# Weights in 512 KB pieces, one account for VectorE's time, tables without GpSimd, final loads one stage ahead

## The chip, the core and the metric

The kernel runs on one core of a Trainium2 chip. The core has TensorE (PE) for matmuls, VectorE (DVE), ScalarE (ACT), GpSimd (POOL) and a queue engine, SyncE (SP); each takes its own instructions in order, and they wait for each other by semaphores. SP, ACT and POOL also start DMA transfers. The metric is the device time of one execution in microseconds (us), lower is better.

## What is computed

One decoder block on 512 tokens of width 2048, in float32, and then a final norm:

```python
h = rmsnorm(x, norm1_g);  z = h @ w_in                     # 2048 -> 3328
x = x + concat([gated(zu, zv), attention(zq, zk, zvv)]) @ w_out
h2 = rmsnorm(x, norm2_g)
q = h2 @ w_query                                           # 8 heads, two halves of 128
s1, s2 = q[..., 0, :] @ sub_keys[0].T, q[..., 1, :] @ sub_keys[1].T
v1, i1 = top_k(s1, 16); v2, i2 = top_k(s2, 16)
top_v, flat = top_k(v1[:, None] + v2[None, :], 16)         # of 256 sums
experts = i1[flat // 16] * 128 + i2[flat % 16]             # of 16384
gates = softmax(top_v)
a = gelu(h2 . expert_down[experts])
out = rmsnorm(x + sum(gates * a * expert_up[experts]), norm_f_g)
```

Each token has 8 x 16 = 128 experts of its own.

## The kernel before

**Two ways to the experts.** 352 of the 512 tokens (three blocks of 128 less 32) go through all 16384 experts densely: 128 "down" blocks of 128 experts each give activations, which are multiplied by a table of gates (zero for an expert that the token did not choose) and go into 16 "up" chunks of 8 blocks. The first 128 tokens and the last 32 gather their own rows instead: 640 "units" (`unit`, line 688), each a gather of 128 rows of 4 KB started on GpSimd (`fetch_to`, 682) and one operation of 1024 elements on VectorE (696 for down, 708 for up).

**Weights.** `Stream` (93) loads every weight matrix in pieces of 1 MB on SP into two buffers, `LOAD` = 2 ahead (104). Each piece is split in halves of 1024 columns: ScalarE makes the rounded part `whi` (118), VectorE or GpSimd the residual `wlo` (120), and `mm3` (141) multiplies three times for each pair of operands, lines 144 to 146. `get` (127) splits two halves ahead of use. A buffer is loaded anew when both of its halves are split. `on_pool` (181) says by the half's number which residuals are GpSimd's.

**Order.** The program is written out in one order by hand; each engine follows it. Stages: input projection with attention and gating; output projection of block 0 (`project`, 539); query of block 0; output projection of blocks 1 to 3; their query; down blocks 0 to 55; up chunks 0 to 5; then up chunks with the down blocks that they need between them; last the norm of the columns just finished (`rows_out`, 1181), 512 at a time, within the last up chunk. `NPRE` = 56 is the number of down blocks ahead of the first up chunk; their activations go through DRAM (`a_dram`), and `OPEN` = `NPRE` - 5 is the block after which the buffers of the tables are given up.

**Filling.** Small work between the matmuls is put in by two queues. `Filler.tick(budget)` (58) runs steps until their stated costs use up a budget of us given at each call (2.0 for each weight half in the query of block 0, 4.0 in the next stage, 2.4 for each half of a down block). The steps are the choice of the 16 best (`choose`, 585), the decoding of the choice into expert numbers (`decode`, 600), and the gate tables (`table`, 875). `Flow.step` (80), called by `mm3` with the nominal time of its three matmuls (`COL_NS` = 0.4505 ns for a column), runs the units at a fixed rate: one for each 2600, later 5200 and 4800 ns, and from block `OPEN` on at the rate that spreads them over what is left (`pace`, 1220).

**Tables.** A table is made four tokens at a time (`quad`, 889; 88 in all): VectorE compares the second key with `iota` (898), GpSimd multiplies by the gates (901), VectorE (905) or ScalarE (910, 912), by turns, makes the one-hot of the first key; TensorE multiplies them (918), ScalarE copies the result out (931). At block `OPEN` what is left of these steps is run at once (the loop at 1240).

**The end.** After down block 127 `open_last` (1146) and `finish_first` (1195) load the residual rows and the gathered sums of the first block on SP, add and normalize them; `finish_last` (1205) does the same for the last 32 tokens and is the last unit.

## Time and profile before

| | |
|---|---|
| time before, median of 3 runs | 3179.93 us (3173.95 to 3181.99) |
| the profiled execution, its own time | 3170.0 us |
| its span, first to last instruction | 3168.0 us |
| mean granted TensorE clock | 0.959 |
| TensorE busy | 2908.4 us, 92% |
| VectorE, ScalarE, GpSimd busy | 2318.6, 1133.9, 1672.8 us |
| moved by DMA | 801.85 MB, mean 253 GB/s |

The profile is of one execution. Matmuls are pipelined, so TensorE counts as busy while one is in flight; whether it runs at its pace is seen in the number of matmuls in a stretch. The stretches below are cut where the first matmul of each stage starts. A granted clock of 1.00 is 2.4 GHz, one of 0.50 is 1.2 GHz.

### The profile page before, as it was taken

How to read it: one execution, taken by the hardware profiler on the slowest of the kernel's cores; microseconds unless marked ns; L12 is line 12 of the kernel's file. 1: busy time of each engine (PE TensorE's matmuls, PEld its weight loads, DVE VectorE, ACT ScalarE, POOL GpSimd, SP SyncE). 2: the span in 40 equal slices, each digit the busy share in tenths (PEclk: the TensorE clock that was granted, in tenths of full speed). 3: DMA queues.
4: the chain of work that ended last, by engine and by line, in shares of the span. 5: the costliest groups of instructions: out<-in, count | busy, mean ns of one | idle time of the engine just before them, and what ended most of it. 6: DMA issues, size and time to landing. Idle time of an engine off the chain costs nothing. (4 is left out here: it accounts for less than half of the span.)

```text
span 3168.0 us, 43607 instructions
## 1 busy us (share of the span) xinstructions
PE 2908.4 (92%) x16925; PEld 2748.2 (87%) x16925; DVE 2318.6 (73%) x3218; ACT 1133.9 (36%) x1776; POOL 1672.8 (53%) x1071
## 2 busy tenths in 40 slices
PE   7999977888999999888999999999999999999955
PEld 6878755668999999888999999999999998999955
DVE  3126546865999999996778887777877776777744
ACT  3244444323333445453432223332332323323323
POOL 2133133365555778886655656556555565565522
PEclk9999989999999999987999999999999999999978
DMA  4211255575567666656998898888988888888862
GB/s 188 92 68 67 81 216 210 198 286 209 200 229 249 232 223 232 250 212 240 342 360 324 333 344 315 314 304 321 338 307 315 320 310 305 334 317 307 320 243 73
DMA packets 215359, 801.85 MB, mean 253 GB/s; under 512 B 19952, under 2 KB 80688, under 8 KB 165296
## 3 DMA queue, kind: packets, MB, share of 16 engines
q1 hardware_dynamic: 107504, 416.02, 36.3%
q0 software_dynamic: 92160, 335.59, 28.0%
q10 hardware_dynamic: 15488, 47.46, 3.9%
q8 instruction: 132, 2.16, 0.3%
q14 instruction: 75, 0.61, 0.1%
HBM read 753.98 MB, written 45.01 MB: 252 GB/s over the span
## 5 line engine op out<-in xcount | busy, mean ns | idle before, releaser
L120 POOL TENSOR_TENSOR wlo<-wraw,whi 128x1024 fp32r<-128x1024 f32 x269 | 684.3, 2546 | 923.4 <-ACT whi L118 818.5
L118 ACT CAST whi<-wraw 128x1024 fp32r<-128x1024 f32 x692 | 700.8, 1047 | 707.2 <-PE up L145 410.8
L120 DVE TENSOR_TENSOR wlo<-wraw,whi 128x1024 fp32r<-128x1024 f32 x423 | 662.4, 1572 | 306.7 <-ACT whi L118 304.9
L144 PE MATMUL up<-gah,whi 128*128 128x352 f32 x2048 | 668.7, 327 | 48.2 <-ACT whi L118 32.9
L146 PE MATMUL dn<-h2d,wlo 128*128 128x352 f32 x2048 | 670.2, 327 | 36.3 <-POOL wlo L120 25.6
L146 PE MATMUL up<-gah,wlo 128*128 128x352 f32 x2048 | 664.2, 324 | 11.2 <-POOL wlo L120 6.1
L145 PE MATMUL dn<-h2d,whi 128*128 128x352 f32 x2048 | 668.8, 327 | 0.0
L144 PE MATMUL dn<-h2d,whi 128*128 128x352 f32 x2048 | 665.4, 325 | 3.0 <-ACT whi L118 3.0
L145 PE MATMUL up<-gal,whi 128*128 128x352 f32 x2048 | 662.8, 324 | 0.0
L144 PEld LDWEIGHTS up<-gah,whi 128*128 128x128 f32 x2048 | 388.5, 190 | 56.1 <-ACT whi L118 34.0
L146 PEld LDWEIGHTS dn<-h2d,wlo 128*128 128x128 f32 x2048 | 390.0, 190 | 42.9 <-POOL wlo L120 29.8
L146 PEld LDWEIGHTS up<-gah,wlo 128*128 128x128 f32 x2048 | 388.3, 190 | 15.2 <-POOL wlo L120 8.1
L144 PEld LDWEIGHTS dn<-h2d,whi 128*128 128x128 f32 x2048 | 390.6, 191 | 3.3 <-ACT whi L118 3.3
L145 PEld LDWEIGHTS dn<-h2d,whi 128*128 128x128 f32 x2048 | 389.7, 190 | 0.0
L145 PEld LDWEIGHTS up<-gal,whi 128*128 128x128 f32 x2048 | 389.4, 190 | 0.0
L682 POOL DMA_INDIRECT row<-in_down_rows,idx x228 | 276.3, 1212 | 136.9 <-DVE row L696 60.9
L696 DVE SCALAR_TENSOR_TENSOR row<-row,half_row 128x1024 f32<-128x1024 f32 x228 | 273.9, 1211 | 43.7 <-DMA row<-in_down_rows,idx 30.3
L682 POOL DMA_INDIRECT row<-in_up_rows,idx x160 | 183.2, 1145 | 86.5 <-DVE half_row L708 35.7
L901 POOL TENSOR_TENSOR p<-eq,gT 128x1024 fp32r<-128x1024 bf16 x88 | 190.6, 2176 | 44.4 <-DVE eq L898 41.7
L682 POOL DMA_INDIRECT more<-in_up_rows,idx x160 | 170.5, 1066 | 72.2 <-DVE half_row L708 36.2
L708 DVE SCALAR_TENSOR_TENSOR half_row<-more,wgt,half_row 128x1024 f32<-128x1024 f32 x160 | 205.2, 1282 | 1.4
L708 DVE SCALAR_TENSOR_TENSOR half_row<-row,wgt,half_row 128x1024 f32<-128x1024 f32 x156 | 200.2, 1284 | 1.4
(218 smaller groups left out, 3963.5 us busy)
## 6 DMA issues: line engine op xcount, KB each, us to landing
wraw<-in_down SPq DMA_DIRECT2D x128, 1024.0 KB, 6.1
wraw<-in_up SPq DMA_DIRECT2D x128, 1024.0 KB, 6.6
wraw<-in_wout SPq DMA_DIRECT2D x32, 1024.0 KB, 4.8
wraw<-in_wq SPq DMA_DIRECT2D x32, 1024.0 KB, 4.8
wraw<-in_win SPq DMA_DIRECT2D x26, 1024.0 KB, 4.8
g_dram<-stage ACTq DMA_DIRECT2D x22, 1024.0 KB, 6.8
g<-g_dram SPq DMA_DIRECT2D x32, 704.0 KB, 9.7
aa<-a_dram SPq DMA_DIRECT2D x56, 176.0 KB, 9.2
```

The costliest lines, as they stand in the source:

```text
L118: self.nc.scalar.copy(hi, src)
L120: eng.tensor_sub(lo, src, hi.bitcast(F32))
L144: nc.tensor.matmul(ps, wh, xh, start=start, stop=False)
L145: nc.tensor.matmul(ps, wh, xl, start=False, stop=False)
L146: nc.tensor.matmul(ps, wl, xh, start=False, stop=stop)
L682: nc.gpsimd.indirect_dma_start(out=t, out_offset=None, in_=src, in_offset=bass.IndirectOffsetOnAxis(ap=idx[i][:, j, h:h + 1], axis=0))
L696: nc.vector.scalar_tensor_tensor(t, t, 1.0, half_row, op0=OP.mult, op1=OP.mult, accum_out=dots[i][:, j, h:h + 1])
L708: nc.vector.scalar_tensor_tensor(half_row, t, wgt[i][:, j:j + 1], half_row, op0=OP.mult, op1=OP.add)
L901: nc.gpsimd.tensor_tensor(p2, eq[:, :, None, :].to_broadcast([P, 4, 2, P]), hl[:, four, :, None].to_broadcast([P, 4, 2, P]), op=OP.mult)
```

## The change

1. `Stream` loads halves: pieces of 512 KB in four buffers, four ahead; a buffer is loaded anew when its half is split.
2. `Filler` and `Flow` go; `Pace` keeps an account for VectorE. Each `mm3` adds 0.97 of its nominal time (at most 3000 ns may stand), each piece of VectorE work takes off its stated cost. While the account is above zero it runs a unit if one is due (`gap`), else a step of the `hot` queue (choices, and the decoding of block 0). Steps of the `paced` queue (decoding and tables of blocks 1 to 3, 110 in all) run one in a step when `due` has reached `every` and nothing is hot, whatever the account. Residuals after the input projection go to GpSimd when VectorE's account is at or below zero and GpSimd's own is not below zero.
3. A quad makes its product of one-hot and gates in four operations on VectorE, none on GpSimd, and all one-hots of the first key on ScalarE.
4. `NPRE` goes from 56 to 80, so `OPEN` from 51 to 75.
5. The loads of the final norm go from SP to ACT; the work of the first block comes in the second quarter of the last up chunk, that of the last tokens is loaded in the third and done in the fourth. A second set of four buffers takes half of the partial sums.

The core of the diff follows. Left out are the removed classes `Filler` and `Flow`, the removal of their calls and the adapted costs of the steps (1750, 1750, 2950 for a choice; 2500, four times 3900, 1500 for a decoding), and the charges for other VectorE work (690 for a residual row or a transposed quarter, 2600 for a norm, 1060 for a table product, 520 for a sum).

```diff
 NCHUNK = NK // CB
-NPRE = 56
+NPRE = 80
 OPEN = NPRE - 5
 TG = 32
 NTG = TD // TG
...
+class Pace:
+        self.hot, self.paced, self.units = deque(), deque(), deque()
+        self.vector = self.pool = self.wait = self.due = 0.0
+        self.gap = 2600.0
+        self.every = 0.0
+    def spend(self, ns):
+        self.vector -= ns
+    def use_pool(self):
+        if self.vector > 0.0 or self.pool < 0.0:
+            self.vector -= 1250.0
+            return False
+        self.vector -= 500.0
+        self.pool -= 2500.0
+        return True
+    def run(self, q):
+        ns, f = q.popleft()
+        self.vector -= ns
+        r = f()
+        if r is not None:
+            self.later.append(r)
+    def step(self, ns):
+        self.vector = min(self.vector + 0.97 * ns, 3000.0)
+        self.pool = min(self.pool + ns, 3000.0)
+        self.wait += ns
+        self.due += ns
+        if self.paced and self.due >= self.every and not self.hot:
+            self.due -= self.every
+            self.run(self.paced)
+        while self.vector > 0.0:
+            if self.units and self.wait >= self.gap:
+                self.wait = max(self.wait - self.gap, -self.gap) if self.wait < 2 * self.gap else 0.0
+                self.vector -= 1260.0
+                self.pool -= 1100.0
+                self.units.popleft()()
+            elif self.hot:
+                self.run(self.hot)
+            else:
+                break
+    def turn(self):
...
+    def finish(self):
+        while self.hot or self.paced or self.later:
+            self.turn()
+            while self.hot:
+                self.run(self.hot)
+            while self.paced:
+                self.run(self.paced)
...
     def drain(self):
+        while self.units:
+            self.units.popleft()()
...
-    LOAD, SPLIT = 2, 2
+    LOAD, SPLIT = 4, 2
...
-        while self.loaded < min(n, len(self.chunks)):
-            i = self.loaded
-            self.raw[i] = self.pool.tile([P, 2048], F32, name="wraw", bufs=2)
-            self.nc.sync.dma_start(self.raw[i], self.chunks[i])
+        while self.loaded < min(n, 2 * len(self.chunks)):
+            p = self.loaded
+            self.raw[p] = self.pool.tile([P, 1024], F32, name="wraw", bufs=4)
+            self.nc.sync.dma_start(self.raw[p],
+                                   self.chunks[p // 2][:, (p % 2) * 1024:(p % 2 + 1) * 1024])
             self.loaded += 1
...
-            self.load(p // 2 + 1)
-            src = self.raw[p // 2][:, (p % 2) * 1024:(p % 2 + 1) * 1024]
+            self.load(p + 1)
+            src = self.raw.pop(p)
...
-            if p % 2:
-                del self.raw[p // 2]
-                self.load(p // 2 + 1 + self.LOAD)
+            self.load(p + 1 + self.LOAD)
...
-        flow.step(3 * ps.shape[-1] * COL_NS)
+        pace.step(3 * ps.shape[-1] * COL_NS)
...
-    LEAD, REST, ASK, EXPERTS = 52, 52 + 68, 52 + 96, 52 + 128
 
     def on_pool(p):
-        if p < LEAD:
+        if p < 52:
             return p < 4 or 20 <= p < 36
-        if p < REST:
-            return p % 3 == 2
-        if p < ASK:
-            return p % 2 == 0
-        if p < EXPERTS + 2 * OPEN:
-            return p % 4 != 0 if p < EXPERTS else p % 2 == 0
-        return p % 3 == 0
+        return pace.use_pool()
...
-            flow.q.append(unit(u))
+            pace.units.append(unit(u))
...
-                    for step in choose(psc, key[b], top[b], pos[b], 2 * g + h, s, h):
-                        fill.add(*step)
+                    pace.hot.extend(choose(psc, key[b], top[b], pos[b], 2 * g + h, s, h))
...
         def quad(n):
             def f():
+                turn()
                 t, hl = eT[0]
                 if len(ready) == 4:
                     take()
                 p1 = pear.tile([P, 4, P], F32R, name="p1", bufs=4)
-                eq = pear.tile([P, 4, P], BF16, name="eq", bufs=4)
                 p2 = pear.tile([P, 4, 2, P], F32R, name="p2", bufs=4)
-                four = slice(4 * n, 4 * n + 4)
-                nc.vector.tensor_tensor(eq, iota[:, None, :].to_broadcast([P, 4, P]),
-                                        t[:, 1, four, None].to_broadcast([P, 4, P]),
-                                        op=OP.is_equal)
-                nc.gpsimd.tensor_tensor(p2, eq[:, :, None, :].to_broadcast([P, 4, 2, P]),
-                                        hl[:, four, :, None].to_broadcast([P, 4, 2, P]),
-                                        op=OP.mult)
-                if n % 2 == 0:
-                    nc.vector.tensor_tensor(p1, iota[:, None, :].to_broadcast([P, 4, P]),
-                                            t[:, 0, four, None].to_broadcast([P, 4, P]),
-                                            op=OP.is_equal)
-                else:
-                    for j in range(4):
-                        nc.scalar.activation(p1[:, j, :], iota, AF.Abs, scale=-1.0,
-                                             bias=t[:, 0, 4 * n + j:4 * n + j + 1])
-                    nc.scalar.activation(p1, p1.bitcast(F32), AF.Relu, bias=1.0, scale=-1.0)
+                for j in range(4):
+                    k = 4 * n + j
+                    nc.vector.scalar_tensor_tensor(
+                        p2[:, j], iota[:, None, :].to_broadcast([P, 2, P]), t[:, 1, k:k + 1],
+                        hl[:, k, :, None].to_broadcast([P, 2, P]),
+                        op0=OP.is_equal, op1=OP.mult)
+                for j in range(4):
+                    nc.scalar.activation(p1[:, j, :], iota, AF.Abs, scale=-1.0,
+                                         bias=t[:, 0, 4 * n + j:4 * n + j + 1])
+                nc.scalar.activation(p1, p1.bitcast(F32), AF.Relu, bias=1.0, scale=-1.0)
...
+        plan, waiting = [], []
+            choice, steps = decoding(b)
+            turn, quads = table(b, choice)
+            head = [*steps, (600.0, lambda t=turn: t)]
+            n = len(head) if b == 0 else 0
+            plan += head[:n]
+            if b:
+                at = len(plan) - 24
+                for k, f in enumerate(head):
+                    plan.insert(at + 3 * k, f)
+            plan += [(0.0, lambda: None)] * 0 + [(1900.0, f) for f in quads]
+        pace.paced.extend(plan)
+        pace.every = OPEN * 48 * TD * COL_NS * 0.95 / len(plan)
...
+            if last and q == 1:
+                rest_of_first()
+            if last and q == 2:
+                pace.drain()
+                rest_of_last = finish_last()
+            if last and q == 3:
+                rest_of_last()
             if last and q:
                 rows_out(q - 1)
...
-            nc.sync.dma_start(t, x_dram[b + 1])
+            nc.scalar.dma_start(t, x_dram[b + 1])
...
-        nc.sync.dma_start(y, y_dram[0])
-        nc.sync.dma_start(x, x_dram[0])
-        nc.vector.tensor_add(y, y, x)
-        for q in range(4):
-            square(ND, P, y, q, nc.gpsimd)
-        last_norm(ND, P, y, o_rows[0])
+        nc.scalar.dma_start(y, y_dram[0])
+        nc.scalar.dma_start(x, x_dram[0])
+
+        def rest():
+            nc.vector.tensor_add(y, y, x)
+            for q in range(4):
+                square(ND, P, y, q, nc.gpsimd)
+            last_norm(ND, P, y, o_rows[0])
+        return rest
 
     def finish_last():
...
+    def spread():
         left = sum(2 * 24 for k, i in order if k == "d" and i >= OPEN)
         left += sum(384 for k, i in order if k == "u")
+        pace.gap = (left * TD * COL_NS - 45e3) / len(pace.units)
...
-            while fill.q or fill.later or ready:
-                fill.tick(1e9)
+            pace.finish()
+            while ready:
                 take()
             open_late()
-            pace()
+            spread()
             opening.extend([
...
-            finish_first()
-            flow.q.append(finish_last)
-    flow.drain()
+            rest_of_first = finish_first()
+    pace.drain()
```

## Rows read from the trace of the kernel before

**Rows 1.** The page's part 1: busy time of each engine, its share of the span, and its instructions.

```profile
PE 2908.4 (92%) x16925; PEld 2748.2 (87%) x16925; DVE 2318.6 (73%) x3218; ACT 1133.9 (36%) x1776; POOL 1672.8 (53%) x1071
```

**Rows 2.** Busy time of one stretch: its start and end (us from the span's start) and length, busy us and number of instructions of each engine, granted TensorE clock, busy share of the DMA engines, GB/s. It is one undisturbed up chunk: 384 matmuls of 352 columns.

```profile
2072.00:2133.00 61.00, 61.00 (x384) 61.00 (x383) 44.26 (x46) 18.57 (x23) 33.59 (x26) 1.00 0.82 312
```

**Rows 3.** The same view by stage. In order: output projection of the first token block; its query; output projection of the other three blocks; the first 56 expert-down blocks, and of these the flush of the tables; six expert-up chunks in a row; nine more of these with 72 down blocks between; the last up chunk; the end.

```profile
389.50:491.39 101.89, 75.08 (x283) 54.09 (x282) 53.98 (x52) 47.30 (x62) 35.54 (x14) 0.92 0.60 216
491.39:573.02 81.63, 61.29 (x232) 43.78 (x230) 65.08 (x144) 37.54 (x43) 28.39 (x11) 0.90 0.55 199
573.02:726.36 153.34, 134.00 (x548) 104.23 (x547) 114.13 (x198) 43.54 (x63) 75.71 (x51) 0.93 0.68 251
886.30:1503.60 617.30, 559.72 (x3404) 548.85 (x3403) 573.59 (x748) 283.23 (x585) 457.31 (x238) 0.91 0.66 234
1389.50:1457.20 67.70, 48.74 (x213) 44.47 (x212) 63.89 (x38) 35.08 (x105) 59.11 (x28) 0.54 0.32 128
1503.60:1896.00 392.40, 374.53 (x2306) 368.15 (x2305) 317.55 (x474) 126.86 (x164) 224.55 (x154) 1.00 0.90 341
1896.00:3026.40 1130.40, 1114.15 (x6914) 1109.12 (x6913) 858.39 (x917) 358.11 (x438) 638.42 (x460) 0.99 0.84 317
3026.40:3145.90 119.50, 71.29 (x424) 69.72 (x423) 57.08 (x59) 30.43 (x53) 33.06 (x23) 0.79 0.38 138
3145.90:3168.00 22.10, 1.74 (x13) 1.01 (x10) 6.94 (x13) 5.62 (x9) 2.21 (x6) 0.65 0.36 130
```

**Rows 4.** The timeline of TensorE among the down blocks: the eight products of one quad; and the busy time of these products (matmuls, then weight loads) in the flush.

```profile
1211.23 1.00 PE L918 MATMUL tr<-p,p 128*128 128x128 f32 x8
...
1389.50:1457.20 67.70, 46.95 (x200) 42.84 (x200) 0.54 0.32 128
```

**Rows 5.** DMA: the page's part 6 for the weight pieces of this stage (KB each, median us from issue to landing), and part 3, the queue of SP and ACT that carries all weights and the queue of GpSimd that carries the gathered rows (packets, MB, share of 16 engines over the span).

```profile
q1 hardware_dynamic: 107504, 416.02, 36.3%
q0 software_dynamic: 92160, 335.59, 28.0%
...
wraw<-in_wout SPq DMA_DIRECT2D x32, 1024.0 KB, 4.8
```

**Rows 6.** The timeline of ScalarE in the output projection of the first block: start, duration, engine, line, operation, tiles, count, and in brackets the idle time before with what ended it. Each row is the two casts of one 1 MB weight piece.

```profile
427.49 1.99 ACT L118 CAST whi<-wraw 128x1024 fp32r<-128x1024 f32 x2 [3.90 <-DMA wraw<-in_wout]
430.96 2.00 ACT L118 CAST whi<-wraw 128x1024 fp32r<-128x1024 f32 x2 [1.48 <-DVE wlo L120]
```

**Rows 7.** The timeline of VectorE around the flush of the tables: one alone, then in the steady flush.

```profile
1397.90 0.68 DVE L905 TENSOR_TENSOR p<-iota,eT 128x512 fp32r<-128x512 f32 x1
...
1409.35 2.98 DVE L898 TENSOR_TENSOR eq<-iota,eT 128x512 bf16<-128x512 f32 x2
1412.25 2.38 DVE L905 TENSOR_TENSOR p<-iota,eT 128x512 fp32r<-128x512 f32 x1
```

**Rows 8.** VectorE's timeline at 996 us, a two-input operation of 256 elements, alone; and the page's part 5, the up half of a unit, which has a per-partition factor.

```profile
996.96 0.41 DVE L594 TENSOR_TENSOR cand<-val 128x256 f32<-128x256 f32 x1
...
L708 DVE SCALAR_TENSOR_TENSOR half_row<-more,wgt,half_row 128x1024 f32<-128x1024 f32 x160 | 205.2, 1282 | 1.4
```

**Rows 9.** The page's part 5, the two splits of a weight half: the residual on GpSimd, the cast on ScalarE, the residual on VectorE (busy us, mean ns of one | idle before it).

```profile
L120 POOL TENSOR_TENSOR wlo<-wraw,whi 128x1024 fp32r<-128x1024 f32 x269 | 684.3, 2546 | 923.4 <-ACT whi L118 818.5
L118 ACT CAST whi<-wraw 128x1024 fp32r<-128x1024 f32 x692 | 700.8, 1047 | 707.2 <-PE up L145 410.8
L120 DVE TENSOR_TENSOR wlo<-wraw,whi 128x1024 fp32r<-128x1024 f32 x423 | 662.4, 1572 | 306.7 <-ACT whi L118 304.9
```

**Rows 10.** Waits of VectorE in the output projection of blocks 1 to 3 (573 to 726 us): us in total, times, longest.

```profile
DVE row L696 <- DMA row<-in_down_rows,idx: 28.6, 8, 6.2
```

**Rows 11.** The timeline of ScalarE in the flush, one pass of copies and table building.

```profile
1410.94 0.65 ACT L931 COPY stage<-tr 128x256 f32<-128x256 f32 x2 [2.20 <-PE tr L918]
1411.47 1.28 ACT L910 ACTIVATE p<-iota,eT 128x128 fp32r<-128x128 f32 x4
1412.78 0.63 ACT L912 ACTIVATE p<-p 128x512 fp32r<-128x512 f32 x1
1413.32 0.63 ACT L931 COPY stage<-tr 128x256 f32<-128x256 f32 x2
```

**Rows 12.** The timeline of GpSimd in the flush.

```profile
1411.87 4.51 POOL L901 TENSOR_TENSOR p<-eq,gT 128x1024 fp32r<-128x1024 bf16 x2 [0.69 <-DVE eq L898]
```

**Rows 13.** Busy time of the row gathers (line 682) on GpSimd after the flush: one for each unit.

```profile
1457.20:3020.00 1562.80, 561.90 (x499) 0.99 0.86 323
```

**Rows 14.** The timeline of SP's queue after the last down block, then of VectorE.

```profile
3026.63 2.54 SPq L1158 DMA_DIRECT2D xr<-x_dram  x3
...
3047.19 2.29 DVE L1200 TENSOR_TENSOR yf<-yf,xf 128x2048 f32<-128x2048 f32 x1 [18.45 <-DMA xf<-x_dram]
3056.21 0.75 DVE L1170 TENSOR_SCALAR yf<-yf,rstd 128x1024 f32<-128x1024 f32 x1 [3.52 <-POOL rstd L1168]
...
3087.01 3.70 DVE L1215 TENSOR_TENSOR xf<-xf,more 32x1024 f32<-32x1024 f32 x3 [7.43 <-DMA xf<-x_dram]
...
3100.93 1.27 DVE L1190 TENSOR_TENSOR xr<-dn,xr 128x512 f32<-128x512 f32 x2
```

**Rows 15.** Waits of TensorE from 3020 us to the end.

```profile
PE up L144 <- ACT whi L118: 24.5, 1, 24.5
PE dn L1187 <- DVE xr L1190: 22.6, 4, 21.5
```

108 lines of the change are left out of this document (35 added, 73 removed).

## The prediction

> **What bounds the kernel now.** I read the parts of the page first. TensorE is busy for 92% of the span and no other engine for over 73% [rows 1], so the span is TensorE's work and what it loses. What it cannot lose comes from an undisturbed chunk: 384 matmuls of 352 columns in 61.0 us, 158.9 ns each, 0.451 ns a column [rows 2]; that is the kernel's own `COL_NS`. A block of 48 matmuls is then 7.6 us, with the seams between blocks 7.68. The windows by stage, set against this floor, say where time is lost [rows 3]:
>
> - Output projection of block 0: 101.9 us; its floor is 16 pieces of 2.77 us (12 x 512 columns) and two of 8.3 for the other blocks, 61. Query of block 0: 81.6 against 44.3. Both lose 40% with no engine near full: a loop of latencies. Projection of blocks 1 to 3: 153.3 against 14 x 8.3 = 116.
> - First 56 down blocks: 617.3. Floor: 56 x 7.68 = 430, and 88 quads of eight products, 0.89 each without overlap (eight in 1.00 [rows 4]), 78. So 109 are lost, 44 of them in the flush: 67.7 us at a granted clock of 0.54 hold 25 quads (200 products [rows 4]), 22 us of TensorE's work.
> - Up chunks with 72 down blocks, 392.4 + 1130.4: floor 15 x 61.3 + 72 x 7.68 = 1472, 51 lost.
> - Last up chunk 119.5 against 61.3, then an end of 22.1.
>
> **The early stages: pieces of 512 KB.** A 1 MB piece lands 4.8 us after its issue [rows 5] and then costs two casts in a row (2.0 us [rows 6]) and a residual. 101.9 less 16.6 for the two wide pieces is 5.3 us a piece, 4.8 if I set 0.5 aside for the start of the stage; the query has 81.6 / 16 = 5.1. Casts of one piece can follow the last by 3.5 us [rows 6], but on the average two buffers give no more than a landing time each. SP's and ACT's queue moved 416 MB in 36.3% of 3168 us, 362 GB/s while busy, GpSimd's with its 4 KB rows 378 [rows 5]. So 1 MB needs 2.9 us of engines, the latency beside it is 1.9, and I estimate 512 KB at 1.9 + 1.45 = 3.35 us to landing. A half then holds its buffer for 3.35 + 1.05 (cast) + 1.22 (a residual on VectorE alone: 0.41 for 256 elements, 0.68 for 512 [rows 7, 8], so 0.68 + 2 x 0.27; the mean of 1.57 [rows 9] has waits for GpSimd in it) + 0.3 that I set for handing over = 5.9 us, four buffers: 1.48 a half, 3.0 a piece. TensorE wants 2.77, the queue gives 2.9. I take 3.1 in the projection (14 pieces from 4.8: 24 us) and 3.3 in the query, where choices drive some residuals to GpSimd at 2.5 (16 from 5.1: 29 us): 53 gained. In the projection of blocks 1 to 3, VectorE waits 28.6 us for gathered rows [rows 10], with residuals queued behind. Following the account through the loops, 40 us of choices and 20 of decoding come first now and only 9 units run there, so I take 25 of its 37. The query of blocks 1 to 3 has nothing to give.
>
> The Trainium skill, "DMA: Bandwidth & Descriptors" (Rules for kernel authors), asks for at least 1 MiB in a DMA. Its fit, 2.0 us and bytes by 436 GB/s, gives 4.4 us for 1 MB and 3.2 for 512 KB; the trace has 4.8 for the first. Four in flight would hide this, two would not; that is the third rival.
>
> **The down stage: the paced queue is not paced.** `due` grows in every step from the start of the program and is never set back. When the tables are queued, the matmuls before have put in 288 + 61 + 44 + 116 + 133 = 642 us; `every` is 542 us / 110 = 4.93. All 110 steps are due at once, and only "nothing hot" holds them. At that time 49 choice steps are left (31 and the last group's 18). Account of the next stretch: units 84 x 1260, choices 49 x 2150, residuals sent to GpSimd 64 x 500, in all 243 us of charges, earned at 0.97 in 251: down blocks 0 to 32. Then one paced step follows each `mm3`: 110 steps in 7 blocks, whatever the account.
>
> In this burst each quad's products stand in TensorE's order between two `mm3`, four quads behind their tables, so TensorE cannot run ahead. ScalarE needs for a quad, start to start, 0.53 for the copies, 1.31 and 0.54 for the one-hot: 2.38 us [rows 11], and 26 us more in all for 14 casts, 7 activations and 22 issues, so 2.65. VectorE needs four operations of 256 elements: 0.41 each [rows 8], to 0.48 with what a per-partition factor adds (1.28 against the 1.22 above, rounded up): 1.92 at most. Pieces: decoding of the first block at its own charges 20; 18 quads at 2.65, 48; 14 quads between seven decoding steps, where VectorE has 27 + 20, and 5 for two residuals of GpSimd that hold it off as GpSimd's part of a quad does now (2.25 us of it against 0.68 grown to 2.38 [rows 7, 12]), 52; the same again, 100; 24 quads, 64. Sum 284; TensorE's part in it is 110 x 0.476 + 78 = 131. I take a loss of 150. Bounds: ScalarE alone, 88 x 2.38 + 20 less 131, 98; all in turn (rival 1), 256. The index DMAs of the last tokens (SP) wait here for VectorE; the weights behind them have four loaded halves, over 60 steps, in hand.
>
> After it VectorE's account stands at -187 us: no units until block 69, no loss for 35 blocks, and no flush. In blocks 0 to 31 GpSimd takes nearly every residual, 2.55 us [rows 9] and 84 / 66 gathers of 1.13 [rows 13]: 4.0 for 3.84 of matmuls, 66 x 0.16, some 10 us lost; I take 20, for waits that do not even out. With 5 at the seam to the up chunks as now: 80 x 7.68 + 78 + 20 + 150 + 5 = 867. Before, the same work was 617 + 24 x 7.68 = 801. **Lost: 66.**
>
> The Trainium skill, "SBUF — State Buffer" (Who interferes with whom), has a VectorE operation with two inputs in SBUF and a GpSimd operation that reads SBUF shut each other out for a whole instruction; the trace agrees, with 0.68 and 2.38 us [rows 7, 12]. So by that rule the tables without GpSimd stay exposed to its residuals.
>
> **The up chunks.** Nine come in a row, not six, then six with 48 down blocks. 489 units are left (504 before) for 1378 - 45 us: one in 2.73 us, against 3.13 [rows 13]. DMA was 0.90 busy in the first six [rows 3]; a unit more in ten adds 3 to 4 points. The 24 blocks more through DRAM are 2 x 24 x 0.18 MB, 24 us of the DMA queue beside other work. VectorE's load goes from 0.76 (858 of 1130 [rows 3]) to some 0.84 in the mixed part, in proportion to units and residuals. I keep 4.1 us a chunk for nine, 37, and take 23 for the rest, 60 against 51. **Lost: 9** (-10 to +45).
>
> **The end.** SP issues 5 MB of loads ahead of weights [rows 14], so TensorE waits 24.5 us for a cast that stands behind the first block's norm, which waited 18.5 for its loads; later 21.5 for VectorE, which is in the last tokens' sums and norm from 3087 to 3101 [rows 14, 15]. On ACT the loads cost it six issues of 0.5 to 0.85, 4 us, in front of casts that have 7.6 us in hand; weights keep SP. The work itself stays in VectorE's order ahead of `rows_out`: 9.7 us (3047.2 to 3056.9) for the first block, 14 for the last tokens, less the 4.7 that TensorE still has before it needs VectorE: 5.5 + 10, and 10 for casts, landing loads and a lower clock. The sums of the last tokens are loaded 23 us before the end of the chunk, the units end by 45: if they were late, ACT and SP would wait for their write, with 15 us of weights in hand. 61 + 25 + 22 = 108 against 141.6. **Gained: 33** (20 to 48).
>
> **Sum**, on the profiled span: 3168 - 53 - 25 + 66 + 9 - 33 = 3132. The profiled execution took 3170.0, 2 more than its span, and the median of the three runs is 0.3% above it: 3134 x 1.0031 = **3144**.
>
> **Rivals.**
> 1. *The burst goes by turns.* If TensorE at half clock (0.54 was granted around the flush) needs 2 x 0.89 = 1.8 us for a quad's products, and ScalarE's copies and one-hots take turns with it, a quad costs 1.8 + 2.4 = 4.2 instead of the 3.0 that the pieces above come to: 88 x 1.2 = 106 more, **3250**, slower. It decides from 3.5 us a quad, 45 us in all. For it: in the flush ScalarE stood idle 2.2 us for products [rows 11]. Against: there the products waited for GpSimd's tables; now tables are to run four quads ahead.
> 2. *The steps are spread after all* (a quad hides nearly all its cost): loss 15, not 150: **3009**. Against it stands the sum of `due`.
> 3. *Halves gain nothing early*: if, as now, only two pieces are effectively in flight, a half takes 5.9 / 2 = 2.95, a piece 5.9: 30 lost instead of 53 gained, **3227**. It speaks for it that pieces overlap little now; against, that the buffer, not the queue, holds back the next issue.
>
> **How the numbers follow.** Chances: forecast 0.60, rival 1 0.17, rival 2 0.08, rival 3 0.10, others 0.05. About 0.3% is what a measurement tells from no change: faster is below 3170, slower above 3189. Within the forecast the terms move by +-20 (early), -52 to +50 (burst), -19 to +36 (ups), +-14 (end), not all one way: 3070 to 3225, of which I give 0.72 to faster, 0.13 to same, 0.15 to slower. Faster: 0.43 + 0.08 + 0.03 = 0.54; same 0.10; slower 0.09 + 0.16 + 0.10 + 0.01 = 0.36. The range leaves out rival 2 and what lies beyond rival 1: 3060 to 3250.
>
> **What would show it.** In the profile after: casts in the first projection every 1.5 us; some 7 blocks near the 33rd down block with ScalarE full, TensorE half busy, all 88 quads and no unit; then 35 blocks without units at 7.68 us; no flush; about 490 units after block 74; waits of 5 and 10 us for `rows_out` at the end. Quads spread over 75 blocks, or losses in the 35 quiet ones, would make the prediction wrong.

## The result and the profile after

The kernel after takes 3195.41 us (median of 5 runs, 3193.5 to 3199.38) against 3176.11 for the kernel before on the same chip (5 runs): ratio 1.0059, 95% interval 1.0045 to 1.0074. It is 0.6% slower, where about 1% faster was forecast. The profiled span went from 3168.0 to 3196.5 us. The page's part 1 answers to [rows 1]; under it two lines of its part 2, ScalarE's busy tenths and the granted clock in 40 slices of 80 us:

```profile
PE 2946.9 (92%) x16925; PEld 2786.5 (87%) x16925; DVE 2187.5 (68%) x3435; ACT 1213.2 (38%) x1996; POOL 1468.0 (46%) x986
...
ACT  3244545323333369953323332222233323233232
...
PEclk9999999989999977689999999999999999999987
```

VectorE and GpSimd have less to do, as meant, and the kernel takes longer all the same. The windows by stage say where. They answer to [rows 3], cut in the same way; the down blocks are in three parts (before, in and after the paced steps), now 80 ahead of the first up chunk, and nine up chunks in a row come next:

```profile
389.00:482.02 93.02, 74.45 (x283) 54.16 (x282) 62.02 (x63) 48.18 (x62) 3.12 (x3) 0.91 0.72 241
482.02:547.50 65.48, 53.89 (x232) 40.18 (x231) 45.61 (x72) 37.98 (x43) 28.76 (x12) 0.97 0.72 245
547.50:693.85 146.35, 131.17 (x549) 103.25 (x547) 112.85 (x228) 43.78 (x63) 76.67 (x41) 0.94 0.57 201
851.04:1114.10 263.06, 257.31 (x1588) 254.94 (x1587) 215.49 (x561) 84.46 (x101) 229.19 (x144) 0.99 0.90 313
1114.10:1379.40 265.30, 206.54 (x1019) 193.46 (x1018) 222.49 (x432) 226.56 (x631) 50.17 (x18) 0.68 0.34 123
1379.40:1702.18 322.78, 313.94 (x1954) 312.91 (x1954) 63.27 (x86) 106.77 (x147) 181.07 (x93) 0.99 0.63 217
1702.18:2313.33 611.15, 574.40 (x3458) 565.91 (x3457) 492.87 (x656) 187.60 (x236) 345.25 (x241) 0.97 0.91 333
2313.33:3067.30 753.97, 742.99 (x4610) 739.74 (x4609) 638.89 (x720) 240.82 (x294) 331.49 (x277) 0.99 0.93 337
3067.30:3174.39 107.09, 76.03 (x424) 73.17 (x423) 67.59 (x74) 30.21 (x53) 29.86 (x26) 0.84 0.52 195
3174.39:3196.50 22.11, 1.73 (x12) 1.00 (x10) 6.94 (x13) 5.62 (x9) 2.21 (x6) 0.60 0.36 130
```

Against [rows 3], in the terms of the forecast's sum (the down blocks of before with 24 x 7.68 = 184.3 moved to them from the mixed part):

| term | forecast | before | after | measured |
|---|---|---|---|---|
| projection and query of block 0 | -53 | 183.5 | 158.5 | -25 |
| projection of blocks 1 to 3, and their query | -25 | 313.3 | 303.5 | -10 |
| 80 down blocks | +66 | 801.6 | 851.1 | +50 |
| up chunks with 48 down blocks | +9 | 1338.5 | 1365.1 | +27 |
| end | -33 | 141.6 | 129.2 | -12 |
| sum, with 0.5 less ahead of them | -36 | | | +29 |

So the burst of tables is there, and is a little cheaper than forecast. The sign was lost elsewhere: the three gains that were to pay for it came to 47 us instead of 111, and the up chunks cost 18 more than forecast.

**The burst.** Between 1114.1 and 1379.4 ScalarE is busy for 226.56 of 265.30 us, the granted clock is 0.68, and seven down blocks pass. TensorE's products and VectorE's four operations of a quad in that window (line, engine, operation, tiles, count, busy us, mean ns, idle before it and what ended that):

```profile
L921 PE MATMUL tr<-p,p 128*128 128x128 f32 x672 | 129.5, 354 | 38.0 <-ACT p L915 27.8 <-DVE p L908 4.7 <-DVE gT L895 4.2
...
L908 DVE SCALAR_TENSOR_TENSOR p<-iota,eT,gT 128x256 fp32r<-128x256 f32 x352 | 162.9, 534 | 23.8 <-PE tr L921 23.5
```

672 products are 84 quads, and with 7 x 7.68 for the blocks and 84 x 0.89 for the products [rows 4], 265.3 less 129 leaves some 137 lost. TensorE stands idle for 59 of these (265.30 less 206.54), for ScalarE's one-hots above all (27.8); the other 78 are matmuls that take longer, at the granted clock of 0.68: it is busy 206.54 us for work of 129. ScalarE's copies of the products in the same window never wait for one:

```profile
L934 ACT COPY stage<-tr 128x256 f32<-128x256 f32 x165 | 51.9, 366 | 0.0
```

**The nine up chunks.** TensorE's waits in 1702 to 2313 us, first for the accumulators, then for residuals:

```profile
L163 PE MATMUL up<-gah,whi 128*128 128x352 f32 x1152 | 379.7, 330 | 13.4 <-DVE accT L1143 13.2
L165 PE MATMUL up<-gah,wlo 128*128 128x352 f32 x1151 | 378.2, 329 | 23.4 <-POOL wlo L142 23.4
```

23.4 us for GpSimd's residuals is new. In the six up chunks in a row of the kernel before it was 1.8:

```profile
L146 PE MATMUL up<-gah,wlo 128*128 128x352 f32 x768 | 248.2, 323 | 6.4 <-DVE wlo L120 4.5 <-POOL wlo L120 1.8
```

GpSimd's timeline in one such place of the kernel after, and TensorE's wait that ended when the second residual was done:

```profile
1774.12 2.42 POOL L142 TENSOR_TENSOR wlo<-wraw,whi 128x1024 fp32r<-128x1024 f32 x1
1776.70 1.81 POOL L697 DMA_INDIRECT row<-in_down_rows,idx  x1 [0.16 <-DVE more L711]
1778.82 0.94 POOL L697 DMA_INDIRECT row<-in_down_rows,idx  x1 [0.30 <-DVE wlo L142]
1779.78 2.35 POOL L142 TENSOR_TENSOR wlo<-wraw,whi 128x1024 fp32r<-128x1024 f32 x1
```

```profile
1782.18 0.66 PE L165 MATMUL up<-gah,wlo 128*128 128x352 f32 x1 [4.36 <-POOL wlo L142]
```

Two residuals follow each other on GpSimd, with two gathers between them that had waited for VectorE, for 0.16 and 0.30 us. Three readings offer themselves: GpSimd is simply slow for a residual; the gathers in front wait for VectorE; the account bunches the residuals. The runs below tell them apart.

**Early.** SP's queue and ScalarE in the first projection: two halves are issued at 434.30 and 435.43, and the casts that wait for them start at 439.34 and 440.69 (the half before had been issued at 430.60 and was cast at 437.36).

```profile
434.30 0.33 SPq L129 DMA_DIRECT2D wraw<-in_wout  x1
...
435.43 0.33 SPq L129 DMA_DIRECT2D wraw<-in_wout  x1
```

```profile
437.36 1.04 ACT L140 CAST whi<-wraw 128x1024 fp32r<-128x1024 f32 x1 [0.46 <-PE acc L165]
439.34 1.05 ACT L140 CAST whi<-wraw 128x1024 fp32r<-128x1024 f32 x1 [0.93 <-DMA wraw<-in_wout]
440.69 1.05 ACT L140 CAST whi<-wraw 128x1024 fp32r<-128x1024 f32 x1 [0.30 <-DMA wraw<-in_wout]
442.43 1.05 ACT L140 CAST whi<-wraw 128x1024 fp32r<-128x1024 f32 x1 [0.69 <-DMA wraw<-in_wout]
445.10 1.05 ACT L140 CAST whi<-wraw 128x1024 fp32r<-128x1024 f32 x1 [1.61 <-DMA wraw<-in_wout]
```

That is 5.0 and 5.3 us to landing, and (445.10 - 437.36) / 4 = 1.94 us from cast to cast. They are no exception: in the two stages of block 0, 33 of 68 casts waited for their load, and these started 5.3 us after its issue (median).

**The end.** ScalarE's queue, VectorE and TensorE in the last up chunk:

```profile
3073.70 0.49 ACTq L1208 DMA_DIRECT2D xf<-x_dram  x1
```

```profile
3102.81 2.29 DVE L1211 TENSOR_TENSOR yf<-yf,xf 128x2048 f32<-128x2048 f32 x1 [8.56 <-DMA xf<-x_dram]
...
3111.82 0.76 DVE L1179 TENSOR_SCALAR yf<-yf,rstd 128x1024 f32<-128x1024 f32 x1 [3.51 <-POOL rstd L1177]
3112.49 1.28 DVE L1199 TENSOR_TENSOR xr<-dn,xr 128x512 f32<-128x512 f32 x2
```

```profile
3113.23 1.09 PE L1196 MATMUL dn<-ident,accT 128*96 128x128 f32 x4 [15.21 <-DVE xr L1199]
```

The loads ended VectorE's idle 8.56 us at 3102.81, the norm of the first block kept it until 3112.49, and only then came the rows for which TensorE had stood 15.21 us.

### The profile page after: what moved, and what is told of

Its sections match the earlier page's. It is cut to its first block, busy times and chain, and to the rows that moved or that the text cites. A ratio compares the mean times of both kernels' runs of the same rounds, so it can differ in the third digit from the quotient of the medians.

```text
span 3196.5 us, 44804 instructions
## 1 busy us (share of the span) xinstructions
PE 2946.9 (92%) x16925; PEld 2786.5 (87%) x16925; DVE 2187.5 (68%) x3435; ACT 1213.2 (38%) x1996; POOL 1468.0 (46%) x986
## 5 line engine op out<-in xcount | busy, mean ns | idle before, releaser
L142 POOL TENSOR_TENSOR wlo<-wraw,whi 128x1024 fp32r<-128x1024 f32 x272 | 674.6, 2490 | 775.2 <-ACT whi L140 700.8
L142 DVE TENSOR_TENSOR wlo<-wraw,whi 128x1024 fp32r<-128x1024 f32 x420 | 548.8, 1313 | 506.1 <-ACT whi L140 500.2
L163 PE MATMUL dn<-h2d,whi 128*128 128x352 f32 x2048 | 676.2, 330 | 10.1 <-ACT whi L140 10.1
L164 PE MATMUL dn<-h2d,whi 128*128 128x352 f32 x2048 | 674.5, 329 | 0.0
L163 PEld LDWEIGHTS dn<-h2d,whi 128*128 128x128 f32 x2048 | 395.7, 193 | 10.7 <-ACT whi L140 10.7
L164 PEld LDWEIGHTS dn<-h2d,whi 128*128 128x128 f32 x2048 | 394.8, 193 | 0.0
L711 DVE SCALAR_TENSOR_TENSOR row<-row,half_row 128x1024 f32<-128x1024 f32 x236 | 282.9, 1212 | 87.9 <-DMA row<-in_down_rows,idx 76.4
L697 POOL DMA_INDIRECT row<-in_down_rows,idx x236 | 257.2, 1090 | 178.6 <-DVE row L711 132.3
L697 POOL DMA_INDIRECT row<-in_up_rows,idx x160 | 190.0, 1188 | 194.8 <-DVE half_row L723 162.1
L697 POOL DMA_INDIRECT more<-in_up_rows,idx x160 | 186.9, 1168 | 180.1 <-DVE half_row L723 153.1
L908 DVE SCALAR_TENSOR_TENSOR p<-iota,eT,gT 128x256 fp32r<-128x256 f32 x352 | 162.9, 534 | 23.8 <-PE tr L921 23.5
```

The costliest lines, as they stand in the source:

```text
L142: eng.tensor_sub(lo, src, hi.bitcast(F32))
L163: nc.tensor.matmul(ps, wh, xh, start=start, stop=False)
L164: nc.tensor.matmul(ps, wh, xl, start=False, stop=False)
L697: nc.gpsimd.indirect_dma_start(out=t, out_offset=None, in_=src, in_offset=bass.IndirectOffsetOnAxis(ap=idx[i][:, j, h:h + 1], axis=0))
L711: nc.vector.scalar_tensor_tensor(t, t, 1.0, half_row, op0=OP.mult, op1=OP.mult, accum_out=dots[i][:, j, h:h + 1])
L908: nc.vector.scalar_tensor_tensor(p2[:, j], iota[:, None, :].to_broadcast([P, 2, P]), t[:, 1, k:k + 1], hl[:, k, :, None].to_broadcast([P, ...
```

## The experiments

The theory after the result had four parts: the burst is the price of a `due` that is never set back; a half lands later than forecast; GpSimd's residuals are late in the up chunks; norm work stands ahead of the rows at the end. Times are medians; ratios are to the kernel before, timed beside each (3175.68, 3177.52 and 3175.82 us in the three groups). "Of after" compares with 3195.41.

**e1_paced: the paced steps spread.**

```diff
-        self.due += ns
+        self.due = 0.0 if self.hot else self.due + ns
-        pace.every = OPEN * 48 * TD * COL_NS * 0.95 / len(plan)
+        pace.every = (OPEN - 34) * 48 * TD * COL_NS * 0.95 / len(plan)
```

> The paced steps now start their due time when the last hot step is done and are spaced 2.69 us apart over down blocks 34 to 75, instead of all being due at once. Theory (the 143 us lost in seven blocks are the price of putting ScalarE's 2.65 us a quad on a TensorE that has only 0.48 us of other matmuls between two quads): 110 steps spread over some 300 us hide nearly all of it, 20 to 50 us stay lost, so the kernel takes 3195 - 143 + 35 = 3087 us, 3060 to 3115, and ScalarE is under 9 tenths in every slice. Rival (a quad costs its 1.6 us wherever it stands, because its products wait for tables in TensorE's order): at least 3150 us.

3095.84 us, ratio 0.9737 (0.9716 to 0.9758): 99.6 less than after. The 80 down blocks take 724.5 us instead of 851.1. The window of the paced steps, and products and quads in it:

```profile
1127.10:1515.10 388.00, 375.40 (x2538) 374.51 (x2538) 339.39 (x453) 310.88 (x745) 215.57 (x94) 0.98 0.58 199
```

```profile
L921 PE MATMUL tr<-p,p 128*128 128x128 f32 x704 | 88.3, 268 | 0.0
...
L908 DVE SCALAR_TENSOR_TENSOR p<-iota,eT,gT 128x256 fp32r<-128x256 f32 x352 | 262.2, 811 | 19.3 <-PE tr L921 18.7
```

All 88 quads, and TensorE waits 0.0 us for any of them. The rival, a price that a quad has wherever it stands, is out. The down blocks are 32 us above their floor (80 x 7.68 + 78), within the 20 to 50 expected. 27 of the gain are missing against 126.6 in the down blocks: the nine up chunks take 628.4 (611.2 in after), where waits for GpSimd's residuals grow to 36.7 us; the rest is 7 in the mixed part and 3 at the end.

**e2_halves_only: the kernel before with `LOAD` = 4 and halves in four buffers.**

```diff
-            self.raw[i] = self.pool.tile([P, 2048], F32, name="wraw", bufs=2)
+            self.raw[p] = self.pool.tile([P, 1024], F32, name="wraw", bufs=4)
```

> The kernel before with one part of the change: 512 KB pieces, four in flight. Theory (a half needs 4.2 to 5.3 us to land when four are in flight, so a cast comes every 1.9 us and not every 1.5): 10 to 40 us faster than the kernel before, of which 25 in the first two stages, some 3150 us. Rival (halves are worth the 78 us that were predicted for all projections, and the account's choices took the rest away in the kernel after): 3100 us or less. Second rival (the halves cost later, by twice as many transfers in the up chunks, what they gain early): 3176 within 10.

3154.52 us, ratio 0.9935 (0.9916 to 0.9954). The stages of [rows 3] again, projection and query of block 0, and the projection of the others:

```profile
389.55:483.26 93.71, 71.92 (x284) 51.64 (x282) 54.42 (x52) 48.31 (x62) 34.59 (x14) 0.95 0.67 228
483.26:558.97 75.71, 57.93 (x231) 42.17 (x230) 61.68 (x143) 38.15 (x43) 25.91 (x11) 0.91 0.64 218
558.97:715.45 156.48, 133.24 (x549) 103.96 (x547) 114.22 (x199) 43.58 (x63) 76.80 (x51) 0.93 0.70 246
```

Alone, halves give 14 us in the first two stages and nothing in the third. They cost nothing later: the 15 up chunks with their 72 down blocks take 1512.3 us, 1522.8 before. Of the 25 of the kernel after, 10 are in the query, 75.7 to 65.5, where VectorE has 143 instructions here and 72 there: that part goes with the account, which puts the choices off. No run had the account without the halves.

**e7_half_bytes: half the bytes, all of the casts and residuals.**

```diff
+            m = 512 if 52 <= p < 120 else 1024
-                                   self.chunks[p // 2][:, (p % 2) * 1024:(p % 2 + 1) * 1024])
+                                   self.chunks[p // 2][:, (p % 2) * 1024:(p % 2) * 1024 + m])
```

> The kernel after, but in the output projection and the query of block 0 each piece loads only 256 KB and its second half repeats the first (so these weights are not the reference's); casts, residuals and products are as many as before. Theory (these two stages are bound by the landing of bytes, a half every 1.9 us): they fall from 158.7 us to 125 to 140, and the kernel after gains 18 to 35 us, 3160 to 3177. Rival (they are bound by a latency that does not depend on bytes, or by the order of casts, residuals and products): they stay above 150, and the time above 3187.

3176.09 us, ratio 0.9994 (0.9984 to 1.0005), 19.3 less than after: the gain is at the lower edge of what the theory gave, the two stages are just outside it.

```profile
389.45:471.55 82.10, 68.97 (x284) 52.66 (x282) 61.01 (x63) 47.26 (x62) 3.12 (x3) 0.94 0.54 167
471.55:532.12 60.57, 51.83 (x231) 39.24 (x229) 48.20 (x72) 37.19 (x43) 28.82 (x12) 1.00 0.49 140
```

The two stages fall from 158.5 to 142.7 us. Half the bytes are worth 16 of the 53 that they stand above their floor (61 + 44.3). The other half is still there, so the 37 that stay are not all free of loads; but 13 casts wait for a load now, for 18 us in all, where 33 had waited 39.5. TensorE is idle for 22 us of the two stages and busy 121 for a floor of 105, and which of the order of casts and residuals, the clock (0.94 in the projection) and the loads that are left holds it was not separated. More buffers were not tried.

**e3_no_pool_late: no residual on GpSimd from the first up chunk on.**

```diff
+        if late:
+            pace.spend(1250.0)
+            return False
         return pace.use_pool()
```

> From the first up chunk on no residual is given to GpSimd; VectorE takes them all and its account is charged 1250 ns for each. Theory (GpSimd's residual stands behind a gather that waits for VectorE's unit, and TensorE waits 23.4 us for such pieces in the first nine up chunks): these waits go, units come less often, 15 to 25 us faster than the kernel after, some 3175 us. Rival (VectorE has no room: its residuals and its part of the up projections queue up, and TensorE waits for VectorE instead): the time stays within 5 us or grows, 3190 to 3215, with more than 13 us of waits for the accumulators' first step.

3195.65 us, ratio 1.0062 (1.0043 to 1.008): no change in the sum, and two large ones inside. TensorE's waits in the nine up chunks, and the waits of the last one:

```profile
L163 PE MATMUL up<-gah,whi 128*128 128x352 f32 x1152 | 373.6, 324 | 12.9 <-DVE accT L1146 12.1 <-ACT whi L140 0.8
L165 PE MATMUL up<-gah,wlo 128*128 128x352 f32 x1152 | 371.9, 323 | 2.3 <-DVE wlo L142 2.2
```

```profile
PE dn L1199 <- DVE xr L1202: 67.9, 4, 41.6
ACT hst L730 <- DVE half_row L726: 47.5, 2, 43.6
```

The nine chunks take 573.2 instead of 611.2 us; the last takes 148.3 instead of 107.1, because VectorE now does units later: 45 of them run in the last chunk, 16 in after, and ScalarE's copy of their last sum waits 43.6 us, with the casts and loads behind it in ScalarE's order. GpSimd's residuals were the cause in the nine chunks; taking them all away moved the bill to the end.

**e5_fetch_less: gathers five units ahead, not seven,** so that each waits for an older unit.

```diff
-            fetch_to(u + 4 + (MORE_ROWS - 1 if "p" in late else 0))
+            fetch_to(u + 4 + (MORE_ROWS - 3 if "p" in late else 0))
```

> The kernel after, with gathers issued five units ahead of VectorE instead of seven in the up chunks, so that a gather waits for a unit that VectorE was given three units earlier; GpSimd keeps its residuals. Theory (GpSimd's residual is late because a gather ahead of it waits for VectorE's unit): TensorE's 23.4 us of waits for GpSimd's residuals in the first nine up chunks fall below 8 and the kernel gains 20 to 40 us, as it gained 38 in those chunks when GpSimd had no residuals: some 3165. Rival 1 (GpSimd's residual is simply slow, 2.4 us, wherever it stands): within 5 us of 3195. Rival 2 (rows land too late with five in flight): VectorE waits over 40 us for rows in those chunks, and the time is 3195 or more.

3226.25 us, ratio 1.0144 (1.0122 to 1.0167): my theory fell. In the nine chunks TensorE waits as long for GpSimd's residuals as before, and longer for the accumulators, since VectorE now waits for rows (the largest of four such groups, of 43.5 us in all, stands last):

```profile
L163 PE MATMUL up<-gah,whi 128*128 128x352 f32 x1152 | 382.3, 332 | 30.3 <-DVE accT L1143 30.3
L165 PE MATMUL up<-gah,wlo 128*128 128x352 f32 x1152 | 380.5, 330 | 26.9 <-POOL wlo L142 26.9
```

```profile
L711 DVE SCALAR_TENSOR_TENSOR more<-more,half_row 128x1024 f32<-128x1024 f32 x48 | 57.7, 1215 | 18.7 <-DMA more<-in_down_rows,idx 18.7
```

The gathers do wait less for VectorE, 21 us in all in these chunks instead of 59, and the residuals come no earlier. So what the gathers wait for is not it, and rival 2 holds as well: five rows ahead are too few here.

**e9_third: every third residual on GpSimd,** as before the change; in the nine chunks the number of them stays (48, not 50, of 144).

```diff
+        if late:
+            pace.spend(500.0 if p % 3 == 0 else 1250.0)
+            return p % 3 == 0
         return pace.use_pool()
```

> The kernel after, but from the first up chunk on every third residual is given to GpSimd, as in the kernel before, instead of by the account; the share is the same third (50 of 144 pieces in the first nine up chunks by the account, 48 by the rule). Theory (the account bunches GpSimd's residuals, two or three of 2.4 us in a row with gathers between them, in the quarters where VectorE and ScalarE prepare the next blocks, so that they come late; five gathers ahead instead of seven did not change that): TensorE's 23.4 us of waits for GpSimd's residuals in the first nine up chunks fall below 8, those chunks from 611 to 575 to 590, and since the units stay in time the kernel gains 20 to 38 us, some 3165. Rival (each GpSimd residual in an up chunk is late, bunched or not): 16 us or more of these waits stay, 3185 or more.

3169.4 us, ratio 0.9983 (0.9971 to 0.9995), 26 less than after. The nine chunks take 582.2 us:

```profile
L163 PE MATMUL up<-gah,whi 128*128 128x352 f32 x1152 | 377.1, 327 | 13.9 <-DVE accT L1146 13.8
L165 PE MATMUL up<-gah,wlo 128*128 128x352 f32 x1152 | 374.4, 325 | 3.2 <-DVE wlo L142 2.2 <-POOL wlo L142 1.0
```

1.0 us of waits for GpSimd instead of 23.4, with as many residuals of 2.5 us and as many gathers in the same queue. So it is not how many residuals GpSimd gets but which: the account sends them just where VectorE is in debt, two or three in a row. e9 changes both at once, so whether the row or the moment makes them late is not shown. Behind the nine chunks the rule gives GpSimd 69 residuals where the account gave 4, and that costs little (756.7 us in the mixed part, 754.0 in after; 136.4 against 129.2 at the end). The first 48 of the nine chunks by engine (P GpSimd, v VectorE), in after and in e9_third:

```
PPvvPvvvvvvvvvvPPPvvPvvvvPvvvvvPvPvPPvvvvPvvvvvP
vPvvPvvPvvPvvPvvPvvPvvPvvPvvPvvPvvPvvPvvPvvPvvPv
```

**e4_rows_first: rows ahead of the norm work.**

```diff
             if last and q == 2:
                 pace.drain()
-                rest_of_last = finish_last()
-            if last and q == 3:
-                rest_of_last()
             if last and q:
                 rows_out(q - 1)
+            if last and q == 2:
+                rest_of_first()
+            if last and q == 3:
+                rest_of_last()
```

(`finish_last` comes at the end of that quarter, and `rest_of_first` leaves the second.)

> In the last chunk the rows of a quarter are written out ahead of the norm work of the first block and of the last tokens, and that work moves one quarter later; nothing else changes. Theory (22.9 us of TensorE's waits for rows in the last chunk, the longest 15.2 and 6.8, come of norm work that stands ahead of them in VectorE's order): 12 to 20 us faster than the kernel after, some 3179 us. Rival (the same work then delays the residual steps of the next pieces, or lengthens the tail): within 4 us of the kernel after.

3185.74 us, ratio 1.0038 (1.0022 to 1.0054), 9.7 less than after: between the two. The last chunk and the end:

```profile
3060.56:3149.53 88.97, 71.37 (x421) 67.75 (x420) 58.77 (x61) 26.58 (x44) 32.96 (x24) 0.92 0.62 232
3149.53:3182.50 32.97, 3.65 (x13) 2.12 (x12) 16.72 (x27) 9.65 (x18) 2.95 (x8) 0.54 0.28 95
```

18.1 gained in the chunk, 10.9 given back behind it, where the work of the last tokens now stands ahead of the last sums.

**e12_loads_sp: rows and first block loaded on SP again** (`nc.scalar.dma_start` to `nc.sync.dma_start` in `open_last` and `finish_first`).

> The kernel after with the last stage's loads of rows and of the first block issued on SP's queue, ahead of the weights, as in the kernel before, at the same place in the program. Theory (ScalarE's queue spares TensorE the wait for weights that come behind 4 MB of loads): TensorE waits 10 us or more for a cast in the last chunk, 8 to 20 us slower than the kernel after. Rival (what counts is when the first block's loads land, 29 us after their issue on ScalarE's queue, since VectorE stands 8.6 us waiting for them ahead of the rows): they land sooner, and the time is within 5 us or better.

3191.74 us, ratio 1.0053 (1.0032 to 1.0074): no difference to after, as the rival had it. The waits of the last chunk and the end:

```profile
PE dn L1196 <- DVE xr L1199: 32.0, 4, 24.0
...
ACT whi L140 <- DMA wraw<-in_up: 24.9, 2, 23.5
```

The cast waits for weights behind the loads, as in the kernel before [rows 15], and through VectorE's order TensorE waits 24.0 for rows in the place of 15.21. The end is 131.9 us, against 129.2. These 2.7 are no gain that the runs can tell: ahead of the down blocks, where the two kernels are the same, the profiled executions differ by 6.1 (845.0 and 851.0), and by the medians the loads on SP are 3.7 faster.

**Together.** All four start from e1_paced and e4_rows_first. e6_nine adds no GpSimd residual in the first nine up chunks, and units spread to end 100 us ahead (`- 100e3` for `- 45e3`); e8_paced_rows_fetch adds five gathers ahead; e10_paced_rows_third adds every third residual; e11_paced_rows_third_gap adds both every third residual and `- 100e3`.

> The kernel after with the paced steps spaced over blocks 34 to 75, rows of the last chunk ahead of the norm work, no residual on GpSimd in the first nine up chunks only, and units set to end 100 us ahead of the last chunk's end by their gap instead of 45. Theory (the three losses are separate and add up; the lateness of the units that cost 41 us at the end when GpSimd had no residuals at all is made good in the mixed part): 3096 - 55 in the nine chunks - 12 at the end = 3030, 3015 to 3055. Rival (units still late: VectorE has no time to give): the last chunk waits for them, 3065 or more.

> The kernel after with the paced steps spaced over blocks 34 to 75, rows of the last chunk ahead of the norm work, and gathers five units ahead; GpSimd keeps its residuals. Theory (as for gathers five ahead alone, and the three losses add up): 3096 - 45 - 12 = 3039, 3025 to 3060, and the units end in time. Rival (rows late with five in flight, or GpSimd slow wherever the residual stands): 3084 within 8, what the first two edits give.

> The kernel after with the paced steps spaced over blocks 34 to 75, rows of the last chunk ahead of the norm work, and every third residual on GpSimd from the first up chunk on. Theory: 3096 - 12 at the end - 35 to 55 in the nine chunks = 3040, 3025 to 3055, with no wait for late units at the end. Rival (as for every third alone): 3070 or more.

> As the one before, with the units set to end 100 us ahead of the last chunk's end by their gap instead of 45. Theory (VectorE has room once GpSimd takes a third): the units end some 40 us earlier, and the time is the same within 6 us, or up to 15 better if they were late. Rival (more units in an up chunk delay VectorE's residuals and the accumulators): 8 us or more worse.

| kernel | us | ratio (interval) | nine up chunks, us |
|---|---|---|---|
| e6_nine | 3046.79 | 0.9581 (0.9559 to 0.9602) | 570.1 |
| e8_paced_rows_fetch | 3106.59 | 0.9771 (0.9748 to 0.9793) | 649.7 |
| e10_paced_rows_third | 3043.72 | 0.9576 (0.9555 to 0.9597) | 581.7 |
| e11_paced_rows_third_gap | 3039.14 | 0.9568 (0.9547 to 0.9588) | 582.7 |

e8 fell with e5: 3025 to 3060 was expected, and its rival had 3084. The others came out within what was expected. In e6 ScalarE still waits 26.2 us at the end for late units; e10 and e11 have a third of the residuals on GpSimd and nearly the same time. e11 beats the kernel before by 4.3% and the kernel after by 4.9%.

## Why the prediction was wrong

**Right: the down stage.** The paced steps stood together as the sum of `due` said: seven blocks from the 34th on, then 30 without units ("until block 69" was forecast, and 35 in the list of signs; the next unit runs at 1611.6 us), and no flush. "I take a loss of 150" measured 137, the stretch ahead of it 263.06 - 33 x 7.68 = 10 for "I take 20", the rest, with the seam, 12 for 5. Rival 1 did not come: 265.3 / 84 is 3.16 us a quad, short of its 3.5, and ScalarE was 85% busy, 2.70 us a quad for the 2.65 forecast. Its condition came in part, a clock of 0.68, but ScalarE's copies did not take turns with the products: they waited 0.0 us for them. The forecast's 131 us of TensorE's part had no term for the clock. Rival 2 describes what e1 built, and there its claim is true: spread, a quad costs nothing beyond its products.

**The step that failed first: "I estimate 512 KB at 1.9 + 1.45 = 3.35 us to landing".** With four in flight a half landed after 5.0 and 5.3. The estimate took a half's bytes at the full rate of the engines, 1.45 us, as if it were alone. By the same figure a half that stands behind others waits 1.45 for each; that this makes the difference is argued, not shown, though with half the bytes the casts that waited started 3.4 us after the issue (e7, median). With 5.1 the buffer is held 5.1 + 1.05 + 1.22 + 0.3 = 7.7, so 1.9 a half (measured 1.94) and 3.8 a piece, not 3.0. And "101.9 less 16.6 ... is 5.3 a piece" took for latency what was partly clock: TensorE was busy 75.08 us there for a floor of 61 [rows 3], and still 74.45 after. Halves alone gave 14 of 53 (e2); some 10 more in the query go with the account, uncredited. The projection of block 0 gained 9 where 24 was forecast, the query 16 for 29. Rival 3, 30 lost, did not come.

The Trainium skill, "DMA: Bandwidth & Descriptors" (Rules for kernel authors), which asks for 1 MiB in a DMA, was weighed with the answer that four in flight would hide the difference. By e2 the halves did gain 14 us in the two stages, so the rule did not decide the sign here, and they hid less than I took. The Trainium skill gives the fit beside it on the same page (Anatomy of one DMA — SWDGE (gpsimd) path) for transfers that GpSimd issues; the 3.2 us worked out from it for 512 KB are about as far from the 5.0 and 5.3 of SP's queue here as the 3.35.

"So I take 25 of its 37", in the projection of blocks 1 to 3, gave 7. VectorE's waits for rows did fall, from 28.6 to 13.4 us, but TensorE was idle for only 19 of the 153.3 us before and for 15 after; it was busy 134.00 and then 131.17 for a floor of 116 [rows 3]. Half of the 37 was not idle time at all.

**The second: "I keep 4.1 us a chunk for nine, 37".** It was 611.15 - 9 x 61.3 = 59. The loads on the queues and VectorE's share were costed; that the account picks *when* GpSimd gets a residual was not. The fixed third of before had spread them without my seeing what it was worth: e9 gives 29 of the 59 back, and the mixed part lost 18 for the 23 taken.

**The third: "5.5 + 10" for VectorE's work at the end.** One wait alone was 15.21, and all four 22.9. The "10 for casts, landing loads and a lower clock" was too small as well: the chunk took 107.09 for 61, and TensorE was busy for 76.03 of it, 15 above the floor, at a clock of 0.84. The loads were taken as landed in time; VectorE idled 8.56 for them until 3102.81, 29 us after their issue at 3073.18 and 3073.70 on ScalarE. e12 shows that the 24.5 us ascribed to SP's order were no gain of their own: with the loads back on SP the end takes 131.9 us, not 24 more than 129.2. Take that wait away, and the work that follows waits for rows.

What stays open: the 37 us above the floor in the first two stages that half the bytes leave, whether it is the row or the moment that makes GpSimd's residuals late, and why e1 raises the waits for them from 23.4 to 36.7.

## What to carry to other kernels

A budget that grows while its consumer is held back is no pace: follow the counter through the whole program to the point where its work is let go. An account that moves work to the slower engine when the faster one is in debt can do so in bunches, at the tightest place, as here; a fixed rhythm of the same share cost less. And before a stall is booked as a gain, name who stands behind it in the same engine's order, and book what the clock takes apart from the waits: it came back with them in the nine chunks (16 of e3's 38 us) and hardly at all in the first projection (75.08 us busy before, 74.45 after).

## What the runs showed of the hardware

Waits of TensorE cost more than their length. Behind the wait of 4.36 us that ended at 1782.18 the granted clock is 0.50, 1.2 GHz, and 13 matmuls run in 3.8 us; in the 4 us after that it is back at 2.4 GHz, and 27 run:

```profile
1782.20:1786.00 3.80, 3.80 (x13) 3.80 (x14) 0.52 (x1) 0.00 (x0) 2.83 (x3) 0.50 1.01 404
1786.00:1790.00 4.00, 4.00 (x27) 4.00 (x26) 2.95 (x5) 0.45 (x1) 1.87 (x2) 0.99 0.97 327
```

In the nine up chunks e3 saves 38.0 us against after, of which the two groups of waits are 21.6 (36.8 to 15.2). The other 16.4 are TensorE's busy time, 558.0 instead of 574.4 us for the same matmuls, at a granted clock of 0.99 for 0.97.

VectorE's operation of 256 elements took 534 ns on the mean in the burst, where GpSimd was busy 50 of 265 us, and 811 when spread, where it was busy 216 of 388. That is 352 x 0.277 = 98 us of VectorE's time for the same work, and TensorE waited none of it. The mean hides two kinds. In e1_paced (shortest, median and longest in ns):

```profile
L908 DVE SCALAR_TENSOR_TENSOR p<-iota,eT,gT x352: 467/474/2703, 1146.0 to 1503.7; 128x256 fp32r<-128x256 f32 x176
```

291 of the 352 took 0.47 to 0.49 us. The other 61 took 1.1 to 2.7, every one of them beside a residual of GpSimd, and 58 of them ended 0.28 to 0.29 us after that residual did; of the 216 with no residual beside them, 38 of these with a gather, none took over 0.49. The Trainium skill, "SBUF — State Buffer" (Who interferes with whom), has such operations shut each other out for a whole instruction; the trace agrees, with these numbers.
